# A hybrid decoder layer on one core: the last projections as channel pairs in seven products each

## The chip, the cores and the metric

The kernel runs on one NeuronCore of a Trainium2 chip (trn2). Its engines are TensorE (PE in the profile; its weight loads are PEld), VectorE (DVE), ScalarE (ACT), GpSimd (POOL) and SyncE (SP), which here issues all DMAs. The metric is the device time of one execution in microseconds, lower is better.

## What is computed

One layer on x, 1,024 positions by 1,024 channels, float32:

```
h = RMSNorm(x)
q,k,v,z_a | u,v_s,z_s | z_m,xBC,dt | gates = split(h @ W_in)
y_att = sliding_window_attention(q,k,v) * silu(z_a)      # 16 heads, window 128
y_sg  = u * (tril(W_s) LN(v_s) + b) * silu(z_s)          # chunks of 128, 8 channel groups
y_ssm = Mamba-2 scan of conv(xBC), dt; * silu(z_m); group RMSNorm   # 4 groups x 8 chunks
merged = sum_i sigmoid(gate_i) * (y_i @ W_br_i)
out = x + RMSNorm(merged @ W_out)
```

## The kernel before

Every float32 operand of a projection is split into a high and a low part in a rounded format (`hi` by a ScalarE cast, `lo` by a VectorE subtraction), and a product is three matmuls: hi x hi, hi x lo and lo x hi. `load_w` (line 76) loads and splits a tile of weights, `raw`, `whi`, `wlo`, with three buffers each. h lies transposed in `hT[0]` and `hT[1]` (high and low). A `ct_unit` (line 88) makes 128 output channels by 1,024 positions: two halves of 512 columns, each 8 k tiles x 3 matmuls into a buffer of `ps_mm`, of which there are three. A `tc_unit` (line 108) makes 128 positions by up to 416 channels, for eight row tiles.

`Stream` (line 133) queues such units and feeds them between other work: `fill(us)` issues steps for so many nominal us, `drain()` the rest; a half of a `ct_unit` counts as 5.2, a row tile of a `tc_unit` as 2.6. TensorE's order is the order in the program. The other engines' instructions and the DMAs are ordered by a planner when the program is built; each engine then runs its list in that order.

The stages are: (1) norm, transposes, and a first `tc_unit` with part of v_s, v and dt; (2) four groups of the scan, each six conv units drained and then a loop over eight chunks, where `decay`, `local`, `scan` and `sums` of the class `Mix` alternate with `st.fill`, and the fill is 5 gate units (6 in the last group) and the next group's four `z_unit`; z goes to two buffers `z2`, one for each half of the positions. (3) Attention in 32 steps with q, z_a and the last gates as fill. (4) A pool `gp`: v_s in three `tc_unit`, layernorm, then for each of eight channel groups `zs_unit`, `u_unit` and `sg_mix`. (5) Four branch passes of eight `ct_unit`, whose right side is y, read back from DRAM by `load_y`: DMA to `yraw` (four buffers), for the scan's y a scaling by `rsb` on POOL, then the cast and the subtraction (on POOL for tiles 4 and 5). The split tiles go to twelve slots; four of them lie in pool `py`, opened before stage 4, the others in `pz`, opened after h is freed. The first unit takes its k tiles as they come. (6) The output projection.

In `decay`, the wait that the change touches, VectorE makes the differences and ScalarE the exponential:

```
for j in range(8):
    V.tensor_scalar(seg[:, j, :], seg[:, j, :], acs[...], 0.0, op0=ALU.subtract, op1=ALU.min)
A.activation(seg, seg, AF.Exp)
```

## Time and profile before

| | |
|---|---|
| three runs, us | 1877.33, 1874.21, 1874.61; median 1874.61 |
| the profiled execution | 1877.33 us, of which the span from first to last instruction 1875.6 |
| mean granted TensorE clock | 0.997 |
| busy share PE / DVE / ACT / POOL | 98% / 55% / 32% / 20% |

Matmuls are pipelined: a busy time of 0.39 us for one of 512 columns is its latency, and its successor starts earlier. The idle time of an engine in a stretch is the stretch less its busy time. PE waits are those in which the engine stood still before an instruction; "<-" names what ended the wait.

### The profile page before, as it was taken

To read this page: it belongs to the slowest core of one execution; us is meant where nothing else is said; L and a number is where in the kernel's file an instruction comes from. 1 tells how busy PE (TensorE), PEld (TensorE's weight loads), DVE (VectorE), ACT (ScalarE), POOL (GpSimd) and SP (SyncE) were. 2 spreads that over 40 slices of the span, in tenths; PEclk is the share of its full clock that TensorE was granted. 3 is DMA by queue.
4 is the path that set the end of the run, shared out by engine and by line. 5 is a ranking of instruction groups with operands and counts; after the bars stand their busy time and mean duration, and the time that the engine had idled before them with its cause. 6 is when DMAs were issued, how large, how long until landed. Compare 5 with 4: busy or idle time off the path is not lost.

```text
span 1875.6 us, 24483 instructions
## 1 busy us (share of the span) xinstructions
PE 1837.7 (98%) x9649; PEld 1555.3 (83%) x9649; DVE 1025.5 (55%) x1653; ACT 599.2 (32%) x1181; POOL 379.0 (20%) x453
## 2 busy tenths in 40 slices
PE   7999999999999999999999999999999999999998
PEld 6888778887888788878888889988887888888898
DVE  6446764667366836685677664533336343534424
ACT  5233333423243324333555553211112021212121
POOL 1001320033003300242466654500003200000000
PEclk9999999999999999999999999999999999999999
DMA  6311441134113521243111114412224453534303
GB/s 207 104 46 56 141 146 45 57 128 154 62 46 102 166 76 46 90 141 114 34 58 46 57 51 157 142 45 68 68 68 152 151 180 94 198 92 135 100 24 135
DMA packets 86755, 186.55 MB, mean 99 GB/s; under 512 B 8528, under 2 KB 41584, under 8 KB 86384
## 3 DMA queue, kind: packets, MB, share of 16 engines
q1 hardware_dynamic: 86640, 184.98, 30.5%
q8 instruction: 76, 1.25, 0.3%
q14 instruction: 39, 0.32, 0.1%
HBM read 149.68 MB, written 35.27 MB: 99 GB/s over the span
## 4 chain that ended last, share of the span: by engine, by line
PE 80%; DVE 8%; issue 4%; ACT 3%; DMA 3%; POOL 2%; SPq 1%; DVEq 0%; POOLq 0%; ACTq 0%
PE ps_mm L100 22%; PE ps_mm L101 22%; PE ps_mm L102 22%; PE ps_mm L126 3%; PE ps_mm L127 3%; PE ps_mm L125 3%; DVE seg L413 1%; PE ps_ac L649 1%; POOL y L470 1%; ACT p L611 1%; DVE seg L438 1%; PE ps_ac L455 1%; DVE ssy L475 1%; ACT whi L82 1%; PE ps_ac L448 1%
## 5 line engine op out<-in xcount | busy, mean ns | idle before, releaser
L100 PE MATMUL ps_mm<-hT,whi 128*128 128x512 f32 x1552 | 612.4, 395 | 0.0
L102 PE MATMUL ps_mm<-hT,wlo 128*128 128x512 f32 x1552 | 604.7, 390 | 0.0
L101 PE MATMUL ps_mm<-hT,whi 128*128 128x512 f32 x1552 | 604.4, 389 | 0.0
L102 PEld LDWEIGHTS ps_mm<-hT,wlo 128*128 128x128 f32 x1552 | 291.3, 188 | 62.0
L100 PEld LDWEIGHTS ps_mm<-hT,whi 128*128 128x128 f32 x1552 | 291.5, 188 | 59.0 <-issue 1.4
L101 PEld LDWEIGHTS ps_mm<-hT,whi 128*128 128x128 f32 x1552 | 291.7, 188 | 57.8
L82 ACT CAST whi<-raw 128x1024 fp32r<-128x1024 f32 (+1 forms) x147 | 153.6, 1046 | 484.6 <-PE ps_mm L101 405.9
L83 DVE TENSOR_TENSOR wlo<-raw,whi 128x1024 fp32r<-128x1024 f32 (+1 forms) x145 | 193.5, 1335 | 200.9 <-ACT whi L82 200.9
L100 PE MATMUL ps_mm<-y,whi 128*128 128x512 f32 x512 | 200.0, 391 | 3.3 <-DVE mg L809 3.3
L101 PE MATMUL ps_mm<-y,whi 128*128 128x512 f32 x512 | 200.0, 391 | 0.6 <-DVE y L788 0.6
L102 PE MATMUL ps_mm<-y,wlo 128*128 128x512 f32 x512 | 199.8, 390 | 0.0
L379 DVE SCALAR_TENSOR_TENSOR acc<-xr,wcv,acc 128x512 f32<-128x512 f32 x144 | 111.3, 773 | 40.2 <-ACT acc L377 36.8
L437 POOL TENSOR_TENSOR y<-xg,dsk 128x512 f32<-128x512 f32 x32 | 38.1, 1202 | 463.0 <-issue 290.5
L100 PEld LDWEIGHTS ps_mm<-y,whi 128*128 128x128 f32 x512 | 96.5, 189 | 23.8 <-DVE mg L809 3.7
L101 PEld LDWEIGHTS ps_mm<-y,whi 128*128 128x128 f32 x512 | 96.4, 188 | 20.9 <-DVE y L788 1.0
L102 PEld LDWEIGHTS ps_mm<-y,wlo 128*128 128x128 f32 x512 | 96.5, 189 | 20.2
L812 DVE SCALAR_TENSOR_TENSOR tm<-gld,ps_mm 128x512 f32<-128x512 f32 x48 | 33.0, 687 | 134.4 <-PE ps_mm L102 134.3
L73 POOL TENSOR_TENSOR rso<-rso,mhalf_row 128x1 f32<-128x1 f32 x8 | 4.3, 542 | 402.5 <-DVE rso L72 402.5
L611 ACT ACTIVATE p<-s,mx 128x129 f32<-128x129 f32 x128 | 50.0, 392 | 101.4 <-DVE mx L607 101.4
L127 PE MATMUL ps_mm<-wlo,hT 128*128 128x256 f32 (+1 forms) x256 | 78.8, 308 | 3.4 <-DVE wlo L83 3.4
L125 PE MATMUL ps_mm<-whi,hT 128*128 128x256 f32 (+1 forms) x256 | 79.7, 311 | 1.5 <-ACT hT L260 1.5
L126 PE MATMUL ps_mm<-whi,hT 128*128 128x256 f32 (+1 forms) x256 | 79.0, 308 | 0.6 <-DVE hT L261 0.6
(184 smaller groups left out, 2583.8 us busy)
## 6 DMA issues: line engine op xcount, KB each, us to landing
seg<-acs_dr SPq DMA_DIRECT2D x32, 512.0 KB, 4.8
yraw<-y_dr SPq DMA_DIRECT2D x32, 512.0 KB, 5.2
raw<-in_w_br_dram SPq DMA_DIRECT2D x32, 512.0 KB, 4.3
gld<-gate_dr SPq DMA_DIRECT2D x32, 512.0 KB, 3.5
raw<-in_w_xbc_dram SPq DMA_DIRECT2D x24, 512.0 KB, 3.6
raw<-in_w_gate_dram SPq DMA_DIRECT2D x24, 512.0 KB, 3.6
gate_dr<-gt SPq DMA_DIRECT2D x48, 256.0 KB, 2.0
raw<-in_w_zm_dram SPq DMA_DIRECT2D x16, 512.0 KB, 5.0
```

The lines of the kernel that those rows point to most:

```text
L82: A.copy(hi, raw)
L83: eng.tensor_tensor(lo, raw, hi.bitcast(F32), op=ALU.subtract)
L100: T.matmul(ps, lhsT=whi[:, ks], rhs=rhs(0, kt, half), start=kt == 0, stop=False)
L101: T.matmul(ps, lhsT=whi[:, ks], rhs=rhs(1, kt, half), start=False, stop=False)
L102: T.matmul(ps, lhsT=wlo[:, ks], rhs=rhs(0, kt, half), start=False, stop=kt == KT - 1)
L125: T.matmul(o, lhsT=lhs(0, kt, tt), rhs=whi[:, ks], start=kt == 0, stop=False)
L126: T.matmul(o, lhsT=lhs(1, kt, tt), rhs=whi[:, ks], start=False, stop=False)
L127: T.matmul(o, lhsT=lhs(0, kt, tt), rhs=wlo[:, ks], start=False, stop=kt == KT - 1)
L379: V.scalar_tensor_tensor(acc, xr[:, k + f0:k + f0 + 512], wcv[:, ti, k:k + 1], acc, op0=ALU.mult, op1=ALU.add)
L437: G.tensor_tensor(d["y"], xg[g][:, :, cs], col(dsk, g), op=ALU.mult)
L611: A.activation(p[:, k, :], s4[:, k, :], AF.Exp, bias=mx[:, k:k + 1], accum_out=den[:, k:k + 1])
L812: V.scalar_tensor_tensor(tm, gt[0][:, fs], 1.0, ps, op0=ALU.add, op1=ALU.mult)
```

## The change

u and z_s, and the second twelve of the 24 gate tiles, are made after attention as 14 pairs of channel tiles. A pair is a product of 256 channels x 1,024 inputs with 1,024 x 1,024 positions, cut into 2 x 2 blocks, and the four output blocks come from seven block products in place of eight (Winograd's form of Strassen's method). The sums of weight blocks are made on POOL as weights come (T1 to T4), the sums of h once, on POOL, with their splits in new tiles S1, S2, S4 (the fourth overwrites a block of h), and the products are added up on VectorE, ScalarE and POOL. A new class `PairStream` issues one product of 12 matmuls at a time and prepares operands four products ahead.

The scan's loop gets 2 gate units and the four z units as fill (6 gates in the last group), in fills of 2.2 for 2.6. v_s moves into attention, where the last gates were, and goes through DRAM; its statistics are kept in `bst`, its norm is applied group by group when it is read back. The differences of `decay` move from VectorE to ScalarE, as a relu with a bias. `py` is opened after the last channel group, and the first three y are loaded while the gate pairs run; `yraw` has two buffers instead of four, and three y slots instead of four lie in `py`. `pz` lies where the S tiles, `ep` and h lay.

The diff, cut to its core:

```diff
+NGATE = 12
+NPY = 3
...
+    class PairStream:
+        AHEAD = 4
...
+        def _load(self, u):
+            raw = []
+            for k in range(2):
+                r = wp.tile([P, 1024], F32, name="raw", tag="raw", bufs=3)
+                nc.sync.dma_start(out=r, in_=self.units[u][0][k])
+                raw.append(r)
+            (r1, r2) = raw
+            self.raw[u] = {"B11": r1[:, 0:512], "B12": r1[:, 512:], "B21": r2[:, 0:512], "B22": r2[:, 512:]}
+        def _sum(self, b, out, x, y, op):
+            b[out] = self.pool.tile([P, 512], F32, name="ts", bufs=3)
+            G.tensor_tensor(b[out], b[x], b[y], op=op)
+        def _prepare(self, q):
+            u, i = divmod(q, 7)
+            while self.loaded <= u:
+                self._load(self.loaded)
+                self.loaded += 1
+            b = self.raw[u]
+            if i == 1:
+                self._sum(b, "T3", "B22", "B12", ALU.subtract)
+                self._sum(b, "T2", "T3", "B11", ALU.add)
+                self._sum(b, "T1", "B12", "B11", ALU.subtract)
+                self._sum(b, "T4", "T2", "B21", ALU.subtract)
+            src = b[("B11", "T2", "B21", "T3", "T1", "T4", "B22")[i]]
+            if q % 2 == 0:
+                self.slot = [wp.tile([P, 1024], F32R, name=n, tag=n, bufs=3) for n in ("whi", "wlo")]
+            hi, lo = (x[:, q % 2 * 512:q % 2 * 512 + 512] for x in self.slot)
+            A.copy(hi, src)
+            V.tensor_tensor(lo, src, hi.bitcast(F32), op=ALU.subtract)
+            self.ops[q] = hi, lo
+            if i == 6:
+                del self.raw[u]
+        def _step(self):
+            n = 7 * len(self.units)
+            if self.done >= n:
+                return None
+            while self.prepared < min(n, self.done + 1 + self.AHEAD):
+                self._prepare(self.prepared)
+                self.prepared += 1
+            u, i = divmod(self.done, 7)
+            hi, lo = self.ops.pop(self.done)
+            self.done += 1
+            if i == 0:
+                self.t = {}
+            t = self.t
+            o = psum(ps_mm, "mm")
+            for kt in range(4):
+                ks = slice(kt * P, (kt + 1) * P)
+                h0, h1 = (self.lhs(i, part, kt) for part in range(2))
+                T.matmul(o, lhsT=hi[:, ks], rhs=h0, start=kt == 0, stop=False)
+                T.matmul(o, lhsT=hi[:, ks], rhs=h1, start=False, stop=False)
+                T.matmul(o, lhsT=lo[:, ks], rhs=h0, start=False, stop=kt == 3)
+            def tmp(name):
+                t[name] = self.pool.tile([P, 512], F32, name="tp", bufs=6)
+                return t[name]
+            dst, evac = self.units[u][1]
+            def block(b, eng, x, y, op=ALU.add):
+                d = dst(b)
+                eng.tensor_tensor(d, x, y, op=op)
+                evac(b, d)
+            if i == 0:
+                A.copy(tmp("s1"), o)
+            elif i == 1:
+                V.tensor_tensor(tmp("u2"), t["s1"], o, op=ALU.add)
+            elif i == 2:
+                block(11, V, t["s1"], o)
+            elif i == 3:
+                V.tensor_tensor(tmp("u3"), t["u2"], o, op=ALU.add)
+            elif i == 4:
+                A.copy(tmp("s5"), o)
+                block(22, G, t["u3"], t["s5"])
+                G.tensor_tensor(t["u2"], t["u2"], t["s5"], op=ALU.add)
+            elif i == 5:
+                block(21, V, t["u3"], o, ALU.subtract)
+            else:
+                block(12, V, t["u2"], o)
+            return 2.8
...
             def first_evac(tt, o):
-                A.copy(vt[:, tt, :], o[:, 0:384])
+                vt = xp.tile([P, 384], F32, name="vt", bufs=3)
+                A.copy(vt, o[:, 0:384])
                 V.tensor_tensor(dtr[:, tt, :], o[:, 384:416], dtb, op=ALU.add)
+                V.bn_stats(bst[:, tt, 0, 0:6], vt[:, 0:256])
+                nc.sync.dma_start(out=vs_dr[:, tt, 0:256], in_=vt[:, 0:256])
+                nc.sync.dma_start(out=v_dr[:, tt, :], in_=vt[:, 256:384])
...
-            nc.sync.dma_start(out=v_dr, in_=vt)
...
                     A.activation(ea, ea, AF.Exp)
                     self.d[c]["ea"] = ea
                 for j in range(8):
-                    V.tensor_scalar(seg[:, j, :], seg[:, j, :], acs[:, c, g * 8 + j:g * 8 + j + 1], 0.0,
-                                    op0=ALU.subtract, op1=ALU.min)
-                A.activation(seg, seg, AF.Exp)
+                    A.activation(seg[:, j, :], seg[:, j, :], AF.Relu, scale=-1.0,
+                                 bias=acs[:, c, g * 8 + j:g * 8 + j + 1])
+                A.activation(seg, seg, AF.Exp, scale=-1.0)
...
-            st.add(*[gate_unit(next(gates), mp) for _ in range(5)])
-            if g == 3:
-                st.add(*[gate_unit(next(gates), mp) for _ in range(1)])
-            else:
+            st.add(*[gate_unit(next(gates), mp) for _ in range(6 if g == 3 else 2)])
+            if g < 3:
                 st.add(*[z_unit(g + 1, j) for j in range(4)])
             mix.decay(0)
             st.fill(10.4)
@@ -498,16 +617,27 @@
                     mix.local(i)
                     if i + 1 < NB:
                         mix.decay(i + 1)
-                st.fill(2.6)
+                st.fill(2.2)
                 if 3 <= i:
                     mix.sums(i - 3)
                 if 1 <= i <= NB:
                     mix.scan(i - 1)
-                st.fill(2.6)
...
+    def vs_unit(qd):
+        def evac(tt, o):
+            vt = vsp.tile([P, 256], F32, name="vst", bufs=3)
+            A.copy(vt, o)
+            V.bn_stats(bst[:, tt, qd, 0:6], o)
+            nc.sync.dma_start(out=vs_dr[:, tt, qd * 256:(qd + 1) * 256], in_=vt)
+        return tc_unit([t["w_vs"][qd - 1][i] for i in range(2)], h_tc, evac, 256)
...
-                        st.add(*[gate_unit(i, ac) for i in gates])
+                        st.add(*[vs_unit(qd) for qd in range(1, 4)])
...
+    es7 = ExitStack()
+    sop = es7.enter_context(tc.tile_pool(name="sop", bufs=1, side="right", reuse_waits="tile"))
+    ep = es7.enter_context(tc.tile_pool(name="ep", bufs=1, side="right", reuse_waits="tile"))
+    sums = {i: [sop.tile([P, 4, 512], F32R, name=f"S{i}{part}") for part in range(2)] for i in (1, 2, 4)}
+    def blk(part, i, j):
+        return hT[part][:, j * 4:(j + 1) * 4, i * 512:(i + 1) * 512]
+    def h_pair(i, part, kt):
+        if i in (1, 4, 6):
+            return sums[{1: 2, 4: 1, 6: 4}[i]][part][:, kt, :]
+        return blk(part, *{0: (0, 0), 2: (0, 1), 3: (1, 0), 5: (1, 1)}[i])[:, kt, :]
+    def split(hi, lo, src):
+        A.copy(hi, src)
+        V.tensor_tensor(lo, src, hi.bitcast(F32), op=ALU.subtract)
+    pst = PairStream(ep, h_pair)
+    with tc.tile_pool(name="bp", bufs=1, reuse_waits="tile") as bp:
+        s3 = [bp.tile([P, 512], F32, name=f"s3{kt}") for kt in range(4)]
+        for kt in range(4):
+            r = {}
+            for i in range(2):
+                for j in range(2):
+                    r[i, j] = bp.tile([P, 512], F32, name=f"r{i}{j}", bufs=2)
+                    G.tensor_tensor(r[i, j], blk(0, i, j)[:, kt, :].bitcast(F32),
+                                    blk(1, i, j)[:, kt, :].bitcast(F32), op=ALU.add)
+            s1, s2, s4 = (bp.tile([P, 512], F32, name=f"s{i}") for i in (1, 2, 4))
+            G.tensor_tensor(s1, r[1, 0], r[1, 1], op=ALU.add)
+            G.tensor_tensor(s2, s1, r[0, 0], op=ALU.subtract)
+            G.tensor_tensor(s3[kt], r[0, 0], r[1, 0], op=ALU.subtract)
+            G.tensor_tensor(s4, r[0, 1], s2, op=ALU.subtract)
+            for i, x in ((1, s1), (2, s2), (4, s4)):
+                split(sums[i][0][:, kt, :], sums[i][1][:, kt, :], x)
+            st.fill(10.4)
         st.drain()
-
-
-    py = ctx.enter_context(tc.tile_pool(name="py", bufs=1, reuse_waits="tile"))
+        for kt in range(4):
+            split(blk(0, 1, 0)[:, kt, :], blk(1, 1, 0)[:, kt, :], s3[kt])
...
+        for c in range(NB):
+            V.bn_aggr(mv[:, c, :], bst[:, c, :, 0:6])
+        V.tensor_scalar(rsv, mv[:, :, 1], EPS, None, op0=ALU.add)
+        G.tensor_tensor(rsv, rsv, mhalf.broadcast_to([P, NB]), op=ALU.pow)
...
+        def zu_unit(g):
+            def dst(b):
+                half, which = b // 10 - 1, zs if b % 10 == 1 else us
+                if which is zs:
+                    zs[g, half] = gp.tile([P, 512], F32, name="zs", bufs=4)
+                else:
+                    us[g, half] = gp.tile([P, 512], F32, name="us", bufs=2)
+                return which[g, half]
+            def evac(b, src):
+                if b in (11, 21):
+                    th = gp.tile([P, 512], F32, name="th", bufs=2)
+                    A.activation(th, src, AF.Tanh, scale=0.5)
+                    V.scalar_tensor_tensor(src, th, 1.0, src, op0=ALU.add, op1=ALU.mult)
+                if b in (12, 21):
+                    half = 0 if b == 12 else 1
+                    V.scalar_tensor_tensor(zs[g, half], us.pop((g, half)), 0.5, zs[g, half],
+                                           op0=ALU.mult, op1=ALU.mult)
+            return [t["w_zu"][g][k] for k in range(2)], (dst, evac)
+        def sg_load(g):
+            gs = slice(g * P, (g + 1) * P)
+            vg = gp.tile([P, NB, P], F32, name="vg", bufs=2)
+            nc.sync.dma_start(out=vg, in_=vs_dr[:, :, gs])
+            w = gp.tile([P, P], F32, name="sgw", bufs=2)
+            nc.sync.dma_start(out=w, in_=t["sg_wT"][:, g, :])
+            bb = gp.tile([P, P], F32, name="sgb", bufs=2)
+            bcast_load(bb, t["sg_b"][gs])
+            G.affine_select(w, w, pattern=[[1, P]], compare_op=ALU.is_ge, fill=0.0, base=0, channel_multiplier=-1)
+            G.tensor_tensor(vg, vg, mv[:, :, 0:1].broadcast_to([P, NB, P]), op=ALU.subtract)
+            V.tensor_tensor(vg, vg, rsv.unsqueeze(2).broadcast_to([P, NB, P]), op=ALU.mult)
+            sg[g] = vg, w, bb
...
+        def gate_pair(n):
+            def tile_(b):
+                return ep.tile([P, 512], F32, name="tp", bufs=6)
+            def evac(b, gt):
+                A.activation(gt, gt, AF.Tanh, scale=0.5)
+                i, half = NGATE + 2 * n + b % 10 - 1, b // 10 - 1
+                nc.sync.dma_start(out=gate_dr[i, :, half * 512:(half + 1) * 512], in_=gt)
+            return [t["w_gp"][n][k] for k in range(2)], (tile_, evac)
+        pst.add(*[zu_unit(g) for g in range(8)])
+        ngp = (24 - NGATE) // 2
+        pst.add(*[gate_pair(n) for n in range(ngp)])
         for g in range(9):
             if g < 8:
-                st.add(zs_unit(g), u_unit(g))
-                st.drain()
+                sg_load(g)
+                pst.fill(2.8 * 3)
             if g > 0:
                 sg_mix(g - 1)
-    ph1.close()
-
-
-    pz = ctx.enter_context(tc.tile_pool(name="pz", bufs=1, reuse_waits="tile"))
-    merged = [pz.tile([P, S], F32, name=f"mg{i}") for i in range(8)]
+            if g < 8:
+                pst.fill(2.8 * 4)
...
-        return [(py if k < 4 else pz).tile([P, S], F32R, name=f"y{i}", tag=f"y{i}_{k}") for i in range(2)]
+        return [(py if k < NPY else pz).tile([P, S], F32R, name=f"y{i}", tag=f"y{i}_{k}") for i in range(2)]
...
-        raw = py.tile([P, S], F32, name="yraw", bufs=4)
+        raw = py.tile([P, S], F32, name="yraw", bufs=2)
...
+    for n in range(NPY):
+        ys[n] = load_y(n)
+    pst.drain()
+    es7.close()
+    ph1.close()
+    pz = ctx.enter_context(tc.tile_pool(name="pz", bufs=1, reuse_waits="tile"))
+    merged = [pz.tile([P, S], F32, name=f"mg{i}") for i in range(8)]
...
-        return ct_unit(t["w_br"][un * 8 + dd], rhs, evac, (4, 5, 6, 7, KT) if un == dd == 0 else (KT,))
-
-    for n in range(8):
+        return ct_unit(t["w_br"][un * 8 + dd], rhs, evac, (3, 4, 5, 6, 7, KT) if un == dd == 0 else (KT,))
+    for n in range(NPY, 8):
```

## Rows read from the trace of the kernel before

**Rows 1.** The page's first part: busy time, share and instructions of each engine.

```profile
PE 1837.7 (98%) x9649; PEld 1555.3 (83%) x9649; DVE 1025.5 (55%) x1653; ACT 599.2 (32%) x1181; POOL 379.0 (20%) x453
```

**Rows 2.** The page's chain that ended last, shares of the span by engine.

```profile
PE 80%; DVE 8%; issue 4%; ACT 3%; DMA 3%; POOL 2%; SPq 1%; DVEq 0%; POOLq 0%; ACTq 0%
```

**Rows 3.** Timeline of TensorE (start, us, instruction): two plain stretches, first and last.

```profile
699.72 0.39 PE L101 MATMUL ps_mm<-hT,whi 128*128 128x512 f32 x1
...
705.84 0.39 PE L101 MATMUL ps_mm<-hT,whi 128*128 128x512 f32 x1
...
1194.82 0.28 PE L125 MATMUL ps_mm<-whi,hT 128*128 128x256 f32 x1
...
1197.94 0.28 PE L127 MATMUL ps_mm<-wlo,hT 128*128 128x256 f32 x1
```

**Rows 4.** Busy us by stage: stretch, length, PE, PEld, DVE, ACT, POOL, clock.

```profile
184.00:264.00 80.00, 78.12 (x469) 62.06 (x469) 62.45 (x116) 26.75 (x49) 30.31 (x25) 1.00 0.48 147
...
1140.00:1157.50 17.50, 17.50 (x101) 15.39 (x100) 5.97 (x10) 6.13 (x9) 8.48 (x13) 1.00 0.23 77
...
1233.00:1418.00 185.00, 185.00 (x866) 154.85 (x866) 56.83 (x75) 24.51 (x32) 0.00 (x0) 1.00 0.20 64
1431.00:1460.00 29.00, 25.55 (x104) 20.65 (x105) 18.77 (x13) 6.09 (x6) 17.61 (x7) 0.94 0.75 266
```

**Rows 5.** TensorE's waits: waiting line, releaser, us in total, times, longest.

```profile
PE ps_tr L426 <- ACT ssum L482: 8.8, 12, 1.0
PE ps_mm L127 <- DVE wlo L83: 3.4, 1, 3.4
PE ps_mm L100 <- DVE mg L809: 3.3, 1, 3.3
```

**Rows 6.** VectorE timeline, one chunk; groups of ScalarE (busy, mean ns, idle).

```profile
802.65 1.65 DVE L413 TENSOR_SCALAR seg<-seg,acs 128x128 f32<-128x128 f32 x8
...
L611 ACT ACTIVATE p<-s,mx 128x129 f32<-128x129 f32 x128 | 50.0, 392 | 101.4 <-DVE mx L607 101.4
...
L415 ACT ACTIVATE seg<-seg 128x1024 f32<-128x1024 f32 x32 | 33.9, 1058 | 77.9 <-DVE seg L413 77.9
...
L430 ACT COPY btok<-ps_tr 128x128 f32<-128x128 f32 x32 | 8.5, 266 | 48.5 <-DVE gtm L428 48.5
```

**Rows 7.** Single lines (ns least, median, most); a group of the page (busy, mean).

```profile
L471 DVE TENSOR_TENSOR y<-y,z x32: 680/1104/1521, 198.9 to 856.8; 128x512 f32<-128x512 f32 x32
...
L463 DVE TENSOR_TENSOR st<-st,ps_ac x24: 666/678/689, 206.2 to 845.8; 128x512 f32<-128x512 f32 x24
...
L83 DVE TENSOR_TENSOR wlo<-raw,whi 128x1024 fp32r<-128x1024 f32 (+1 forms) x145 | 193.5, 1335 | 200.9 <-ACT whi L82 200.9
```

**Rows 8.** The chain that ended last, in the pass of the channel groups.

```profile
1394.54 1.78 PE ps_ac L726 x16
```

**Rows 9.** Timeline of TensorE at the entry to the branches.

```profile
1431.16 0.50 PE L101 MATMUL ps_mm<-y,whi 128*128 128x512 f32 x1 [0.59 <-DVE y L788]
...
1453.56 0.59 PE L100 MATMUL ps_mm<-y,whi 128*128 128x512 f32 x1 [3.29 <-DVE mg L809]
...
1456.93 0.54 PE L102 MATMUL ps_mm<-y,wlo 128*128 128x512 f32 x1
```

**Rows 10.** Instructions on tile yraw: count, ns least/median/most, first, last start.

```profile
L787 ACT CAST y<-yraw x32: 1038/1048/1059, 1176.6 to 1687.5; 128x1024 fp32r<-128x1024 f32 x32
L788 DVE TENSOR_TENSOR y<-yraw,y x30: 1200/1219/3418, 1177.7 to 1689.2; 128x1024 fp32r<-128x1024 f32 x30
L785 POOL TENSOR_TENSOR yraw<-yraw,rsb x16: 2376/2408/3384, 1174.2 to 1461.9; 128x1024 f32<-128x1024 f32 x16
L788 POOL TENSOR_TENSOR y<-yraw,y x2: 2475/2660/2845, 1420.0 to 1422.5; 128x1024 fp32r<-128x1024 f32 x2
...
DMA to landing us min/median/max: 3.4/5.2/10.0
```

**Rows 11.** The chain that ended last, in the first stage.

```profile
33.09 3.47 DMA xt<-in_x_dram
```

More of the change, by code (lines that the diff above doesn't have):

```diff
@@ L731, in sg_mix @@
                 ytf = yt.rearrange("p j s -> p (j s)")
-                V.tensor_tensor(ytf, ytf, zs[g][:, half * 512:(half + 1) * 512], op=ALU.mult)
+                V.tensor_tensor(ytf, ytf, zs.pop((g, half)), op=ALU.mult)
                 nc.sync.dma_start(out=y_dr[24 + g, :, half * 512:(half + 1) * 512], in_=ytf)
-        st.add(*[vs_unit(qd) for qd in range(1, 4)])
-        st.fill(5.2)
-        for c in range(NB):
-            nc.sync.dma_start(out=vs[c][:, 0:256], in_=v_dr[:, c, 0:256])
-            V.bn_stats(bst[:, c, 0, :], vs[c][:, 0:256])
@@ L768, in hybrid_kernel @@
+    py = ctx.enter_context(tc.tile_pool(name="py", bufs=1, reuse_waits="tile"))
     spare = {}
```

101 lines of the change are left out of this document (47 added, 54 removed).

## The prediction, made before the change was run

> **What bounds the kernel now.** I read the page first. TensorE is busy 98% of the span and the next engine 55% [rows 1], and the chain that ended last lies 80% on TensorE [rows 2]. A matmul's busy time is a latency that overlaps its neighbour's, so a full TensorE row alone says little; the next view was therefore the start times in a plain stretch of projections. 27 matmuls of 512 columns start in 705.84 - 699.72 = 6.12 us, 0.227 us each [rows 3], and each matmul of that size in the projections and branches costs this much of the path as long as TensorE waits for nobody. The windows by stage show where it does wait [rows 4]: nowhere in the pass that makes u and z_s (185.00 of 185.00), 1.9 us in a scan (one of four is shown), 3.4 us around 1445. TensorE's own list of waits names them [rows 5]: 8.8 us in the four scans for ScalarE's copy of a sum, 3.4 us at the v_s units, 3.3 us in the first branch. So what counts is (a) matmuls taken away, at 0.227 us, (b) waits of TensorE taken away, (c) waits put in. Other engines' work is free until it makes a wait.
>
> **Products: -38.1 us.** u, z_s and twelve gates are 28 tiles, each 2 halves of 24 matmuls. As 14 pairs in seven products of 12 they take 14 x 84 = 1,176 matmuls instead of 14 x 96 = 1,344: 168 x 0.227 = 38.1 us less. Operands keep their size (128x128 against 128x512), so I keep the pace.
>
> **Scan: -5 us (bounds -8.8 to +3).** Per chunk VectorE loses eight subtractions, 1.65 us for the eight as they run back to back [rows 6]. Now ScalarE's exponential waits for them, 77.9 us in total [rows 6], and the small copy that TensorE waits for [rows 5] is on the same engine. Afterwards ScalarE does both steps itself. Its price is not in the trace: from below a 128x128 copy is 0.27 us, from above an activation with a bias column and a sum is 0.39 us on 129 columns [rows 6], which gives 2.1 to 3.1 us a chunk; I take 0.30 each, since the upper row also accumulates. VectorE is busy 62 of 80 us in a scan and ScalarE 27 [rows 4]; 64 x 0.3 = 19 us bring ScalarE to 46, so there is room. Filler moves out of the scan (12 half units in place of 13); that is done elsewhere and costs nothing in itself. One wait is put in on paper: the z units of the next group now start in chunk 3 instead of 8, and their second halves cannot be evacuated until chunk 7 has read the old second half. Counting the fills at 2.2, two such results hold two of the three ps_mm buffers from chunk 4 to 8, the third serves the rest, and the next buffer is asked for after chunk 7's scan. I price it at nothing; with the scan a chunk late it is one evacuation a group, under 2 us. Of the 8.8 us I take 5.
>
> The Trainium skill speaks against this move (ScalarE: Activation LUTs, section "Rules for kernel authors"): relu belongs on VectorE, which is faster per element. By that the step would be 2.4 us against 1.65 a chunk; no run here yet shows the operation on ScalarE.
>
> **Entry to the pairs: -3.4 and +3 us (0 to 10).** The wait at the v_s units goes, since they now fill attention. In its place come the sums of h: POOL makes 32 of 128x512, each half of the 2.41 us of its 1,024-wide product [rows 10], 38.5 us. TensorE's cover is the rest of v_s. At step 28 of attention the queue holds 7.8 + 62.4 nominal us and seven steps take 36.4, so 33.8, or 13 row tiles, are left, each 24 matmuls at 0.12 us (1197.94 - 1194.82 for 26 [rows 3]): 37.4 us, plus the first product, which needs no sum, 2.7 us. POOL is half busy at attention's end (8.48 of 17.50 [rows 4]), so some sums can start early, if the planner places them so; the splits into the S tiles must wait for attention's memory. With 10 us done early there is no wait; with none, T3 and T2 (2.4 us), a cast and a split behind them and VectorE's splits in between, 5 to 10 us. SyncE's load of v_s for group 0 waits for the last v_s write, and the pairs' weights may stand behind it.
>
> **Inside a u/z_s pair: +2 us over all eight (0 to 55).** TensorE: 84 x 0.227 + 18/16 x 1.78 for mixing and bias [rows 8] = 21.0 us. VectorE: 20 steps of 512 at 0.68 (seven splits, five sums with a PSUM input, four of gating, four of mixing) and one 1,024-wide scaling at 1.22: 14.8 us [rows 7, 10]. ScalarE: 11 steps at about half of 1.05 [rows 10]. POOL: 6 x 1.2 + 2.4 = 9.6. TensorE is still the longest, if VectorE's times hold. They need not: with two SBUF inputs y<-y,z takes 0.68 to 1.52 us, median 1.10, and the wide split of y 1.20 to 3.42, while sums with a PSUM input stay within 0.67 and 0.69 [rows 7, 10]. What differs is whether POOL runs beside them. 13 of the 20 steps and the wide one have two SBUF inputs. If half of their delay strikes, as the median of y<-y,z has it, VectorE needs 14.8 + 6.5 = 21.3, 0.3 over TensorE. If they are hit only in proportion, as the weight splits are (1.335 on average against 1.22, 9%, with POOL busy a fifth of the span [rows 1, 7, 10], so some 23% with POOL busy half), 17.1. I take the second, being the larger count, and 2 us for single late operands; they are prepared four products, 10.9 us, ahead.
>
> The Trainium skill calls this a lock (SBUF — State Buffer, section "Who interferes with whom"): a VectorE instruction with two SBUF inputs and a GpSimd one that reads SBUF exclude each other for a whole instruction. The rows agree in kind: 0.84 us more is most of a 1.2 us POOL operation.
>
> In the six gate pairs VectorE has 12 of those steps, 8.2 us, against 19.0 of TensorE: nothing.
>
> **Entry to the branches: +15 us (0 to +20).** Now four of the first eight y are split long before, and the other four lie in four yraw buffers, already scaled; only casts and splits remain, and TensorE waits 0.59 us [rows 9]. After the change three are ready, two lie in the only two yraw buffers, and their targets in pz overlie h and the S tiles, which TensorE reads until the last products. So y5 can be loaded only when y3 or y4 is split. From the end of the pairs (0): y3 is split at 0 to 2.5; then load 5.2 (least 3.4), scaling on POOL 2.41, cast 1.05, split on POOL 2.66 [rows 10]: y5 at 1.2 + 11.3 = 12.5. y7, in y5's or y6's buffer: load, scaling, cast and a split of 1.22 on VectorE, 9.9: 22.4 (17.6 to 25.9). TensorE then does the last 6 matmuls, 1.4 us, and ends the first unit at 23.8 instead of 48 x 0.227 = 10.9: 12.9 us of waiting (8.1 to 16.4), in two gaps of several us. The present 3.29 us gap shows what a gap adds: the eight starts after it lie 0.42 us apart, the lower level of 1.2 GHz, before the pace is 0.227 again [rows 9]; 1.6 us a gap. 12.9 + 3.2 - 0.6 is 15.5; I take 15. The 3.3 us block of VectorE at y8 stays. Nothing is added only if y5 to y7 find buffers earlier than I see.
>
> **First stage: +1.5 us (0 to 4).** One write of v becomes 16, on the queue that feeds x, whose load is on the chain there with 3.5 us [rows 11]; eight statistics join VectorE.
>
> **Sum.** -38.1 - 5 - 3.4 + 3 + 2 + 15 + 1.5 = -25.0. The profiled execution took 1877.33 (span 1875.6 and 1.7 around it) and is the slowest of the three runs: 1852.3. From their median, 1874.61, it is 1849.6. I say 1850.
>
> **Rivals.** (A) As above, 0.56. (B) The branch entry is hidden and the scans lose all waits: 1850 - 15 - 3.8 = 1831. For it: scaling of y began at 1174 before, some 240 us ahead [rows 10]. Against it: two buffers. 0.14. (C) VectorE becomes the pairs' bound: with all 13 steps at 1.52 and the wide one at 3.42 a pair takes 27.9 us against 21.0, 8 x 6.9 - 2 = +53: 1903. It ends slower than before once a pair takes over 21.0 + 26.6/8 = 24.3 us, three quarters of those delays. For it y<-y,z; against it the weight splits, and that nothing but chance puts POOL's work beside VectorE's. 0.10. The Trainium skill's lock (SBUF — State Buffer, same section) is this case when every such pair of instructions meets. (D) ScalarE becomes the scan's pace: 8 x 0.39 + 1.06 in one queue with steps that wait for others, 1 us a chunk over today: 32 us more and the 5 not won, 1887 at full, 1871 at half. For it the 77.9 us that ScalarE already waits in; against it 46 of 80 us. 0.12, mostly at half or less. The Trainium skill's rule on relu (ScalarE: Activation LUTs) would come out here. (E) Nothing is won: sums late by 10, branch entry 20, pairs 10 and scans as now: 1875. 0.08.
>
> **Chances and range.** A measurement of this kernel tells about 0.2% (3.7 us) from no change. Faster: A, B, most of D, half of E, 0.84; same: the rest of E, 0.05; slower: C and the end of D, 0.11. The range leaves out C, D's end and the low end of B: 1830 to 1874. A alone is 1839 to 1861.
>
> **What would show it.** 1,176 pair matmuls 0.227 us apart and 21 us from one mixing to the next; 24.3 or more is C. No wait for ssum's copy: the scan step is right; scans longer than now with less filler: D. No gap before the first product that reads an S tile: the sums were in time. Two gaps of 3 to 8 us in the first branch unit, before y5 and y7: the branch step is right; none: B. The prediction is wrong if TensorE waits elsewhere, above all inside the pairs.

## The result, and the profile after

The changed kernel takes 1918.69 us (median of 4 runs, 1915.50 to 1924.31) where the kernel before takes 1875.97 (4 runs beside it): a ratio of 1.0231, 95% interval 1.0200 to 1.0261. It is slower, against a forecast of 1850 us with a range of 1830 to 1874. The profiled execution took 1924.31 us with a span of 1922.6, 47.0 us longer than the span before.

The first part of its page, and its row of TensorE's granted clock in 40 slices:

```profile
PE 1827.9 (95%) x9481; PEld 1540.4 (80%) x9481; DVE 1101.1 (57%) x1546; ACT 724.5 (38%) x1551; POOL 570.9 (30%) x570
...
PEclk9999999999999999999999989999997999999999
```

TensorE has 9649 - 9481 = 168 instructions less than in [rows 1], just those of the products, but its share fell from 98% to 95%, and two slices show a lower clock where none did. The products' pace, from TensorE's timeline inside a pair:

```profile
1200.99 0.39 PE L247 MATMUL ps_mm<-hT,whi 128*128 128x512 f32 x1
...
1211.89 0.39 PE L247 MATMUL ps_mm<-hT,whi 128*128 128x512 f32 x1
```

48 matmuls in 10.90 us are 0.227 us each, as in [rows 3]. So the saving is there, and more than twice as much is lost to something else. TensorE's waits after (waiting line, releaser, us in total, times, longest), against [rows 5]:

```profile
PE ps_tr L602 <- ACT btok L551: 13.9, 8, 3.4
PE ps_mm L105 <- ACT y L964: 12.3, 3, 7.2
PE ps_mm L130 <- DVE bst L637: 11.8, 2, 7.4
PE ps_tr L375 <- DVE hh L367: 10.4, 3, 7.4
PE ps_mm L130 <- ACT whi L87: 9.8, 1, 9.8
PE ps_mm L247 <- DVE us L259: 6.0, 4, 2.1
```

Only the fourth row (the first norm) was there before at about this size. The others name four places: the scan (btok), the entry to the pairs (the v_s units' L130, for evacuations and for a weight), the pairs (L247), and the branches (L105). The windows by stage of the changed kernel (columns as in [rows 4]), one scan, the entry to the pairs, the pairs, the entry to the branches:

```profile
184.00:264.00 80.00, 75.68 (x455) 59.99 (x453) 51.07 (x70) 37.77 (x92) 29.93 (x24) 0.96 0.38 119
1095.00:1165.00 70.00, 44.27 (x249) 40.55 (x250) 35.10 (x49) 18.76 (x37) 49.06 (x34) 0.80 0.23 67
1165.00:1350.00 185.00, 179.00 (x841) 148.43 (x840) 150.88 (x179) 52.26 (x92) 100.93 (x64) 0.98 0.32 103
1444.00:1480.00 36.00, 21.33 (x66) 15.24 (x65) 11.32 (x9) 8.89 (x10) 16.48 (x8) 0.72 0.62 221
```

A stage loses by its waits and by the lower clock level after them, so I put both in one number. For every two neighbouring TensorE instructions of a trace I take the time between their starts, less the median of that time for the same line and shape; the sum over a stage is its excess. The medians add up to 1811.7 us before and 1776.0 after, 35.7 less: the products. The excess, in us, worked out so for every profiled execution below (in the kernel before, "to pairs" is its v_s units and "pairs" its u and z_s tiles; "to branches" are the first 41 us behind the pairs):

```
                      first  scans  attn  to pairs  pairs  to branches  later
before                 11.4   21.0   4.5     6.4    -0.1      6.5       -0.4
after                  16.2   32.9   6.8    30.2    16.1     21.4        8.4
e1_scan_decay          14.8   43.1   8.3    29.3    19.4     18.5        8.1
e2_entry_sums          15.2   27.6   6.6     0.1    20.2     18.2        7.7
e3_pair_vg_early       11.6   28.1   6.7    30.4    16.9     20.9        8.8
e4_branch_order         9.8   28.8   8.2    29.4    17.7     13.2       12.6
e5_scan_fills          13.9   14.9   6.9    30.4    18.0     17.6        8.4
e6_pair_vg_pool        11.1   28.2   8.2    29.4    11.6     19.0        8.1
e7_pair_no_sums        14.9   29.0   6.8    25.2     6.9     19.3        7.8
e8_yraw_four           12.0   28.4   8.0    30.3    17.5      9.0       -0.5
e9_pair_sums_vec       13.3   28.3   8.2    26.6    15.6     20.2        7.0
e10_all                10.7   13.6   8.3     0.1     5.9      9.9       -0.5
e11_all_sums_vec       11.1   14.7   8.4     0.0    10.1     10.3       -0.5
e12_all_order          11.9   15.6   8.4     0.1     4.1      4.2       -0.5
e13_scan_gates_only    15.7   34.2   8.3    29.0    17.9     18.2        7.3
e14_all_decay          16.0   24.0   8.3     0.1     5.2      4.3       -0.5
```

After less before: +4.8, +11.9, +2.3, +23.8, +16.2, +14.9, +8.8, together 82.7; less 35.7 that is the 47.0 us. Where an experiment left a stage as it is in the changed kernel, attention, the way to the pairs and the later passes repeat within 2 us. The first stage lies between 9.8 and 16.2, the scans between 27.6 and 32.9, the pairs between 16.1 and 20.2, and the way to the branches between 17.6 and 21.4, so smaller differences there say nothing. The trace of the changed kernel has the least of these values for the pairs and the greatest for the branches.

### The profile page after: what moved, and what is told of

Same layout as the page of the kernel before. It is cut to its first block, busy times and chain, and to the rows that moved or that the text cites. A ratio compares the mean times of both kernels' runs of the same rounds, so it can differ in the third digit from the quotient of the medians.

```text
span 1922.6 us, 24786 instructions
## 1 busy us (share of the span) xinstructions
PE 1827.9 (95%) x9481; PEld 1540.4 (80%) x9481; DVE 1101.1 (57%) x1546; ACT 724.5 (38%) x1551; POOL 570.9 (30%) x570
## 5 line engine op out<-in xcount | busy, mean ns | idle before, releaser
L105 PE MATMUL ps_mm<-hT,whi 128*128 128x512 f32 x1104 | 436.6, 395 | 0.8 <-DVE z L317 0.8
L107 PE MATMUL ps_mm<-hT,wlo 128*128 128x512 f32 x1104 | 430.2, 390 | 0.0
L106 PE MATMUL ps_mm<-hT,whi 128*128 128x512 f32 x1104 | 430.1, 390 | 0.0
L87 ACT CAST whi<-raw 128x1024 fp32r<-128x1024 f32 (+1 forms) x119 | 124.1, 1043 | 338.1 <-PE ps_mm L106 317.0
L105 PEld LDWEIGHTS ps_mm<-hT,whi 128*128 128x128 f32 x1104 | 207.4, 188 | 44.3 <-issue 2.5
L107 PEld LDWEIGHTS ps_mm<-hT,wlo 128*128 128x128 f32 x1104 | 207.3, 188 | 44.0
L106 PEld LDWEIGHTS ps_mm<-hT,whi 128*128 128x128 f32 x1104 | 207.7, 188 | 40.9
L88 DVE TENSOR_TENSOR wlo<-raw,whi 128x1024 fp32r<-128x1024 f32 (+1 forms) x117 | 152.2, 1302 | 117.7 <-ACT whi L87 117.6
L105 PE MATMUL ps_mm<-y,whi 128*128 128x512 f32 x512 | 202.8, 396 | 12.3 <-ACT y L964 12.3
L106 PE MATMUL ps_mm<-y,whi 128*128 128x512 f32 x512 | 203.2, 397 | 7.1 <-DVE y L965 3.8
L105 PEld LDWEIGHTS ps_mm<-y,whi 128*128 128x128 f32 x512 | 98.0, 191 | 34.5 <-ACT y L964 14.1
L130 PE MATMUL ps_mm<-whi,hT 128*128 128x256 f32 (+1 forms) x256 | 83.0, 324 | 25.7 <-DVE bst L637 11.8
L247 PE MATMUL ps_mm<-hT,whi 128*128 128x512 f32 x224 | 89.8, 401 | 10.3 <-DVE us L259 6.0
L534 ACT ACTIVATE seg<-seg,acs 128x128 f32<-128x128 f32 x256 | 80.9, 392 | 28.2 <-DMA seg<-acs_dr 28.1
L249 PE MATMUL ps_mm<-hT,wlo 128*128 128x512 f32 x224 | 88.6, 396 | 0.0
```

What stands on the lines that cost most here:

```text
L87: A.copy(hi, raw)
L88: eng.tensor_tensor(lo, raw, hi.bitcast(F32), op=ALU.subtract)
L105: T.matmul(ps, lhsT=whi[:, ks], rhs=rhs(0, kt, half), start=kt == 0, stop=False)
L106: T.matmul(ps, lhsT=whi[:, ks], rhs=rhs(1, kt, half), start=False, stop=False)
L107: T.matmul(ps, lhsT=wlo[:, ks], rhs=rhs(0, kt, half), start=False, stop=kt == KT - 1)
L130: T.matmul(o, lhsT=lhs(0, kt, tt), rhs=whi[:, ks], start=kt == 0, stop=False)
```

## The experiments

Each kernel differs from the changed one as its diff shows. Times stand against 1918.7 us; those of the kernel before, run beside them, were 1875.6 to 1875.9.

**The scan.** First the relus were put back as subtractions (e1_scan_decay).

```
-   A.activation(seg[:, j, :], seg[:, j, :], AF.Relu, scale=-1.0, bias=acs[...])
-   A.activation(seg, seg, AF.Exp, scale=-1.0)
+   V.tensor_scalar(seg[:, j, :], seg[:, j, :], acs[...], 0.0, op0=ALU.subtract, op1=ALU.min)
+   A.activation(seg, seg, AF.Exp)
```

> The scan's segment subtraction is back on VectorE (tensor_scalar, then Exp without the sign), the fills stay at 2.2; all else as in the changed kernel (1918.7 us). Theory: the eight relus of a chunk stand at the head of ScalarE's in-order queue, wait there for the segment's transfer (28.1 us over 19 waits), and btok and the ssum copy wait behind them, which is the 2.4 to 3.4 us wait of TensorE in each group (13.9 us over 8). Then the excess of the four scans falls from 33 us to 21 to 24 us, the waits for btok go, and the time is 1907 to 1911 us. Rival: the smaller fills (2.2 for 2.6) leave chunks with too little work between them, whichever engine subtracts. Then the waits move to a releaser on VectorE and the time stays at 1915 to 1922 us.

1929.7 us (ratio 1.0293, 1.0275 to 1.0310), 11 us slower still; the waits for btok came to 17.0 us where they had been 13.9. My theory fell: the relus help. A wait in the changed kernel, from the timelines of TensorE, ScalarE and VectorE:

```profile
212.67 0.60 PE L547 MATMUL ps_tr<-ident,xg 128*128 128x128 f32 x4
216.46 0.58 PE L602 MATMUL ps_tr<-ones,ssy 128*128 128x1 f32 x2 [3.18 <-ACT btok L551]
```

```profile
207.80 2.45 ACT L534 ACTIVATE seg<-seg,acs 128x128 f32<-128x128 f32 x8 [2.42 <-DMA seg<-acs_dr]
...
213.61 0.69 ACT L534 ACTIVATE seg<-seg,acs 128x128 f32<-128x128 f32 x2 [2.27 <-DMA seg<-acs_dr]
214.21 0.61 ACT L594 ACTIVATE sqj<-y 128x512 f32<-128x512 f32 x1
...
216.14 0.27 ACT L551 COPY btok<-ps_tr 128x128 f32<-128x128 f32 x1 [0.21 <-DVE gtm L549]
```

```profile
214.86 1.05 DVE L596 TENSOR_REDUCE ssy<-sqj 128x128 f32<-128x512 f32 x1 [1.56 <-ACT sqj L594]
215.83 0.28 DVE L549 TENSOR_TENSOR gtm<-ps_tr,gmask 128x128 f32<-128x128 f32 x1
```

Between the transposes (L547) and the sum (L602) of this chunk there is no projection at all, where the kernel before has a half unit in every chunk. ScalarE waits for a transfer, VectorE for ScalarE, and nothing covers it. A chunk's two fills of 2.2 give 4.4 nominal us and a half unit costs 5.2, so in some chunks the first fill issues nothing. In TensorE's trace those with a sum behind their transposes are the fourth and the fifth chunk of each group: eight places in the four groups, and the eight waits for btok lie two in each group. Two runs tested that; the first changes the fills and, so that the work lasts, the gate tiles, the second the gate tiles alone.

```
-   st.add(*[gate_unit(next(gates), mp) for _ in range(6 if g == 3 else 2)])
+   st.add(*[gate_unit(next(gates), mp) for _ in range((3, 3, 4, 6)[g])])    # NGATE = 16
-   st.fill(2.2)      # twice in each chunk; e5_scan_fills only
+   st.fill(2.6)
```

> The scan's fills are 2.6 again (one half unit in each chunk), and the groups have 3, 3, 4 and 6 gate tiles for 2, 2, 2 and 6, so that the work lasts; the relus stay on ScalarE. Four gate tiles thereby go back from two pairs (2 x 19.1 us) to plain tiles (4 x 10.9 us), which costs 5.4 us. All else as in the changed kernel (1918.7 us). Theory: with fills of 2.2 one chunk in six has no half unit between its steps, the segment's buffer and TensorE's transposes then come a half unit too early, and all of the scans' extra 11.6 us comes from there. Then the waits for btok go, the excess of the scans falls from 33 to some 20 us, and the time is 1908 to 1913 us. Rival: ScalarE's eight relus in a row delay btok at any pace of the chunks. Then the waits stay, and the time is 1921 to 1926 us.

> The changed kernel with 3, 3, 4 and 6 gate tiles in the scans, and the fills left at 2.2; so the z units start later, as in the run with fills of 2.6, and the pace is that of the changed kernel. Theory of the pace: the two chunks a group without a half unit stay, the excess of the scans stays at 27 to 32 us, and the time is 1917 to 1923 us. Rival: the z units' second halves, which cannot be evacuated before chunk 7, made the waits. Then the excess falls to some 15 us, and the time is 1904 to 1910 us.

With both: 1906.3 us (1.0166, 1.0150 to 1.0182), 12.4 less, although the four gate tiles that go back to plain form cost 24 matmuls, 5.4 us; the excess of the scans is 14.9, and of TensorE's waits in the scans these are left, none for btok:

```profile
PE ps_tr L547 <- ACT ssum L603: 2.5, 5, 1.1
PE ps_mm L105 <- DVE z L317: 1.1, 2, 0.6
```

With the gates alone: 1925.3 us (1.0262, 1.0238 to 1.0286), excess 34.2, btok 15.7 us in 8 waits. So it is the pace of the fills, not the chunk in which the z units start.

**The entry to the pairs.** POOL's timeline there, the first and the last sums, and what ScalarE waits for from 1075 to 1135:

```profile
1080.51 5.03 POOL L839 TENSOR_TENSOR r<-hT,hT 128x512 f32<-128x512 f32 x4
...
1127.22 1.70 POOL L845 TENSOR_TENSOR s<-r,s 128x512 f32<-128x512 f32 x1
```

```profile
ACT S L828 <- POOL s L842: 18.3, 4, 5.0
ACT S L828 <- POOL s L843: 8.7, 4, 2.3
...
ACT S L828 <- POOL s L845: 7.0, 4, 2.3
```

POOL begins after attention's last step and needs 48 us. ScalarE's queue:

```profile
1088.07 0.62 ACT L828 CAST S<-s 128x512 fp32r<-128x512 f32 x1 [3.67 <-POOL s L842]
1088.60 0.37 ACT L636 COPY vst<-ps_mm 128x256 f32<-128x256 f32 x1
1091.03 0.63 ACT L828 CAST S<-s 128x512 fp32r<-128x512 f32 x1 [2.06 <-POOL s L843]
...
1099.30 0.62 ACT L828 CAST S<-s 128x512 fp32r<-128x512 f32 x1 [4.71 <-POOL s L842]
1099.83 0.36 ACT L636 COPY vst<-ps_mm 128x256 f32<-128x256 f32 x1
1102.19 0.62 ACT L828 CAST S<-s 128x512 fp32r<-128x512 f32 x1 [2.00 <-POOL s L843]
1102.71 1.04 ACT L87 CAST whi<-raw 128x1024 fp32r<-128x1024 f32 x1
```

TensorE's longest wait in this stage:

```profile
1103.81 0.58 PE L130 MATMUL ps_mm<-whi,hT 128*128 128x256 f32 x1 [9.79 <-ACT whi L87]
```

The evacuations (L636) of v_s tiles run only when the cast ahead of them has its sum from POOL; at 1099.83 TensorE had stood still for some 6 us. The cast of the last v_s weights (L87) stands behind two such casts, and it is what TensorE's longest wait is for. So the v_s units, meant as the cover of the sums, are held up by them.

```
-   G.tensor_tensor(r[i, j], ...)      # and s1, s2, s3, s4: 32 in all
+   V.tensor_tensor(r[i, j], ...)
```

> The 32 sums of h blocks at the entry to the pairs run on VectorE instead of POOL; all else as in the changed kernel (1918.7 us). Theory: POOL needs 49 us for its sums (1.29 to 1.7 us each), and the casts and splits that wait for it stand in ScalarE's and VectorE's in-order queues ahead of the evacuations of the v_s projections, so TensorE starves at POOL's pace. With 32 sums at some 0.7 us on VectorE (22 us of its idle time) the excess of 1040 to 1165 us falls from 30 us to 8 to 14 us, and the time is 1897 to 1904 us. Rival: it is the amount of work in front of the evacuations, or the transfers of the weights, and not POOL's pace. Then 22 us more on VectorE leave the waits in place and the time is 1912 us or more.

1888.8 us (1.0077, 1.0051 to 1.0104): 29.9 less, more than the theory said, and the excess at this place is 0.1. The rival fell: VectorE makes the sums besides its own work and TensorE does not wait. The run doesn't tell apart POOL's 1.29 us a sum and the 0.4 us that a split beside it takes longer (1.1 us for 0.69).

**The pairs.** VectorE's groups from 1165 to 1350 (busy, mean ns, idle before and its releaser), changed kernel:

```profile
L225 DVE TENSOR_TENSOR wlo<-ts,whi 128x512 fp32r<-128x512 f32 x33 | 33.1, 1014 | 0.3 <-ACT whi L224 0.3
...
L887 DVE SCALAR_TENSOR_TENSOR zs<-us,zs 128x512 f32<-128x512 f32 x16 | 19.6, 1224 | 1.0
...
L901 DVE TENSOR_TENSOR vg<-vg,rsv 128x1024 f32<-128x1024 f32 x6 | 10.7, 1791 | 19.2 <-POOL vg L900 19.2
...
L259 DVE TENSOR_TENSOR zs<-tp,ps_mm 128x512 f32<-128x512 f32 x15 | 10.2, 678 | 3.7 <-PE ps_mm L249 3.7
```

Two suspects: steps with two SBUF inputs take 1.0 to 1.2 us, while the sum with a PSUM input takes 0.678; and VectorE stands for POOL's vg. Four runs:

```
e3   the DMAs of sg_load(g + 1) issued right after sg_mix(g - 1), the arithmetic left where it was
e6   -  V.tensor_tensor(vg, vg, rsv...)        +  G.tensor_tensor(vg, vg, rsv...)
e7   the four _sum calls left out; T1 to T4 replaced by B11, B12, B22, B12 (other numbers come out)
e9   -  G.tensor_tensor(b[out], b[x], b[y])    +  V.tensor_tensor(b[out], b[x], b[y])
```

> In the pairs, the three transfers of each spatial gate (vg, its matrix, its bias) are issued four products before their arithmetic and not directly ahead of it; all else as in the changed kernel (1918.7 us). Theory: VectorE stands at vg's normalisation (22.3 us over 7 waits) for POOL, which stands for vg's transfer (25.5 us over 3), and with it the evacuations that release TensorE. Then both waits go, the period of a pair falls from 22.9 us to 21.2 to 21.8, and the time is 1907 to 1912 us. Rival: VectorE and POOL slow each other (VectorE's subtraction at 1.0 us for 0.68, POOL's sum at 1.6 for 1.3), so that VectorE is full either way. Then the period stays at 22.4 us or more, and the time at 1914 to 1920 us.

1919.2 us (1.0233, 1.0215 to 1.0252), excess 16.9. This tested nothing: the order in which the program writes the transfers is not the order in SyncE's queue. In e3 vg still stood behind the weights there, and POOL's waits for it are those of the changed kernel (25.7 us for 25.5).

> In the pairs, the second step of vg's normalisation runs on POOL like the first, so that VectorE no longer waits there; all else as in the changed kernel (1918.7 us). (The earlier emission of vg's transfers left their place in SP's queue as it was, behind the weights, and so tested nothing of this.) Theory: VectorE's 22 us at vg are what makes every second pair's evacuation late. Then the period of a pair falls from 22.9 to 21.3 to 21.8 us, and the time is 1908 to 1913 us. Rival: the exclusion of VectorE and POOL makes VectorE full, and POOL has 1.9 us more in each pair. Then the period stays at 22.4 us or more, and the time at 1915 to 1925 us.

1909.3 us (1.0187, 1.0163 to 1.0212), excess 11.6 for 16.1, and 22.0 us from one mixing (the matmuls with sgw) to the next where the changed kernel takes 22.9 (the mean of six, from the starts of L908): the wait at vg is a part, not the whole. VectorE's splits of T sums rose to 1.37 us here, and it waits 12.2 us for a tile (`us`) from POOL instead.

> POOL's four sums of weight blocks in each pair are left out, and the products take plain weight blocks in their place (the products of the pairs are other numbers, as many and as long); all else as in the changed kernel (1918.7 us). Theory of the exclusion: of POOL's 101 us of 185 the sums are 50 us; without them VectorE's splits fall from 1.0 us towards 0.75, the period of a pair falls from 22.9 to 21.1 to 21.6 us, and the time is 1904 to 1910 us. Rival (VectorE's wait at vg alone): POOL reaches vg no earlier, since it waits there for the transfer. Then the period stays at 22.4 us or more, and the time at 1914 to 1920 us.

1902.7 us (1.0144, 1.0129 to 1.0159), 21.1 us from mixing to mixing for 22.9, excess 6.9, of which 5.0 is one late evacuation among the gate pairs. Two groups in the same window:

```profile
L225 DVE TENSOR_TENSOR wlo<-raw,whi 128x512 fp32r<-128x512 f32 x60 | 56.2, 958 | 9.6 <-ACT whi L224 9.6
...
L887 DVE SCALAR_TENSOR_TENSOR zs<-us,zs 128x512 f32<-128x512 f32 x14 | 9.7, 690 | 1.2 <-DVE zs L884 0.5
```

Without the sums L887 takes 0.69 us in place of 1.22, but the splits (L225), which I expected near 0.75, still 0.96: POOL is busy 58.5 us of the window with its other steps. VectorE's busy time in the window fell from 150.9 to 134.3 us, though its own work was the same; its wait at vg from 19.2 to 12.3.

> In the pairs, the four sums of weight blocks run on VectorE and not on POOL; all else as in the changed kernel (1918.7 us). Leaving them out gave a pair of 21.1 us for 22.3 and 1902.7 us. Theory: the pairs lose by the exclusion (VectorE's steps take 1.0 us for 0.68 while POOL adds) and by POOL's pace, not by the amount of work. VectorE then has 2.7 us more work in a pair and gets some 3 to 4 us back on its other steps, the period is 21.1 to 21.6 us, and the time 1903 to 1911 us. Rival: VectorE is nearly full by its own work (18 of 22.3 us a pair), and 2.7 us more make it the bound. Then the period is 22.3 us or more, and the time 1917 to 1930 us.

1911.6 us (1.0192, 1.0176 to 1.0209), excess 15.6, 22.25 us from mixing to mixing: neither theory quite. VectorE's other steps sped up (L887 0.68), but its busy time stayed at 151.9, since the sums took what the exclusion gave back, and it still waited 21.5 us for POOL's vg. So neither the wait at vg (e6) nor POOL's sums on VectorE (e9) mends the pairs alone; without the sums (e7) the pace is TensorE's own, though a wait at vg is left. How the loss divides between the wait and the slower steps, these runs do not show.

**The branches.** Timelines of SyncE, TensorE (its longest wait) and POOL at the entry (the bracket says how long the engine stood still and what ended it):

```profile
1449.03 2.55 SPq L957 DMA_DIRECT2D yraw<-y_dr  x2
...
1463.42 1.41 SPq L957 DMA_DIRECT2D yraw<-y_dr  x2
```

```profile
1459.91 0.79 PE L105 MATMUL ps_mm<-y,whi 128*128 128x512 f32 x1 [7.21 <-ACT y L964]
```

```profile
1456.44 4.65 POOL L962 TENSOR_TENSOR yraw<-yraw,rsb 128x1024 f32<-128x1024 f32 x2 [5.21 <-DMA yraw<-y_dr]
...
1468.70 2.34 POOL L962 TENSOR_TENSOR yraw<-yraw,rsb 128x1024 f32<-128x1024 f32 x1 [5.31 <-DMA yraw<-y_dr]
```

The transfers go two at a time, and the next two 14 us later. Two mends:

```
e4   order = (2, 0, 1, 3): attention's tiles, which L962 doesn't scale, in the first pass
e8   -  NPY = 3, yraw bufs=2, xt2 in a buffer of its own
     +  NPY = 2, yraw bufs=4, xt2 in yraw's buffers
```

> The first pass of the branch projection takes attention's eight tiles, which need no scaling by the row norms on POOL, and the two scaled passes come second and third; all else as in the changed kernel (1918.7 us). Theory: at the entry each tile goes in a row through a transfer (5 us), POOL's scaling (2.4 to 2.7 us), ScalarE's cast and the split, with two buffers for the raw tile; without POOL's step the excess of 1452 to 1480 us falls from 21 us to 10 to 14 us, and the time is 1906 to 1913 us. Rival: the two raw buffers alone set the pace (a transfer is issued only when the split of the tile two before it is done). Then a tile still takes as long as transfer, cast and split, 5 to 6 us for two tiles, the excess stays at 18 us or more, and the time at 1914 to 1922 us.

> Four buffers for the raw branch tiles in place of two, with two tiles (not three) kept ready before the branches for the room; all else as in the changed kernel (1918.7 us). Theory: a tile's transfer is issued only when the split of the tile two before it is done, so transfer (5 us), scaling (2.5 us), cast and split follow each other; with four buffers the transfers run ahead, the waits of the later passes (8.7 us) go, and the excess at the entry falls from 21 to 13 to 18 us: 1902 to 1908 us. Rival: POOL's scaling (2.4 to 2.7 us a tile, after its last work for the pairs) and the casts set the pace. Then the entry stays at 20 us or more, only the later passes gain something, and the time is 1911 to 1918 us.

The order alone: 1912.2 us (1.0199, 1.0182 to 1.0216); the entry went from 21.4 to 13.2, as forecast, but the scaled tiles now come in later passes and lose 12.6 there for 8.4. Four buffers: 1898.6 us (1.0122, 1.0100 to 1.0144), 20.1 less, more than expected; the entry 9.0, the later passes nothing, though one tile less was ready. TensorE's waits from 1425 to 1700 with four:

```profile
PE ps_mm L105 <- ACT y L964: 2.6, 1, 2.6
PE ps_mm L106 <- DVE y L965: 2.6, 2, 1.8
PE ps_mm L106 <- POOL y L965: 1.1, 2, 0.7
```

**Together.** e10_all has the entry's sums on VectorE, the fills of 2.6 with the gate tiles of e5, four raw buffers, and vg's normalisation on ScalarE:

```
-   G.tensor_tensor(vg, vg, mv[:, :, 0:1]..., op=ALU.subtract)
-   V.tensor_tensor(vg, vg, rsv..., op=ALU.mult)
+   for c in range(NB):     # nmr = -mean * rsv, once
+       A.activation(vg[:, c, :], vg[:, c, :], AF.Identity, scale=rsv[:, c:c + 1], bias=nmr[:, c:c + 1])
```

e11_all_sums_vec adds the pair sums on VectorE, e12_all_order the order of e4, and e14_all_decay is e12 with the diff of e1.

> Four mends together on the changed kernel (1918.7 us): the entry's sums on VectorE (measured alone 1888.8 us), the fills of 2.6 with 16 plain gate tiles (1906.3), four raw branch buffers (1898.6), and vg's normalisation on ScalarE in eight activations, which takes 1.9 us a pair from POOL and 1.8 from VectorE. Theory: the four places are apart in time and each wait is local, so the gains add: 1918.7 - 29.9 - 12.4 - 20.1 = 1856, less 3 to 9 us for vg, 1847 to 1853 us; by TensorE's paces (1778 us and an excess of some 12 + 15 + 7 + 2 + 11 + 9) it is 1836 us. So 1836 to 1853 us, below the kernel before. Rival: the waits hide behind one another, or the mends collide at the entry to the pairs and the branches. Then 1862 us or more.

> The four mends together and, besides, the four sums of each pair on VectorE. Theory of the exclusion: 5 to 9 us below the four mends alone, since POOL is left with two steps a pair. Rival: VectorE's own work decides: the same or slower than the four mends alone.

> The four mends together and, besides, attention's tiles in the first pass of the branches. Theory: of the 9 us that are left at the branches' entry with four buffers, POOL's scaling is part, and 3 to 6 us go. Rival: with four buffers the transfers and the casts set the entry, and the time is that of the four mends within 2 us.

> The best version (the four mends and attention's tiles first, 1839.1 us) with the scan's subtraction back on VectorE. The prediction's step: the relus on ScalarE are worth 5 us (0 to 9) at an even pace: 1840 to 1848 us. By what they gave at the uneven pace: 11 us, 1850 us. Rival: at an even pace ScalarE's eight relus cost TensorE as much as VectorE's subtractions: within 2 us of 1839.

e10: 1846.2 us (0.9845, 0.9829 to 0.9861). The gains add; the pairs lose 5.9. e11: 1849.2 us (0.9858, 0.9844 to 0.9871): the rival held; from mixing to mixing it is 21.1 us for 21.5, but the first S products wait for their operands (2.8 and 1.7 us), so nothing is won. e12: 1839.1 us (0.9810, 0.9791 to 0.9828), the best, 36.7 us under the kernel before; with four buffers the order no longer costs later passes anything. The page of e12:

```profile
PE 1804.0 (98%) x9505; PEld 1526.3 (83%) x9505; DVE 1104.2 (60%) x1551; ACT 742.3 (40%) x1601; POOL 485.7 (26%) x518
...
PEclk9999999999999999999999999999999999999999
```

e14: 1852.7 us (0.9869, 0.9849 to 0.9889), one run of four 1844.9. The scans' excess is 24.0 for 15.6, and TensorE's wait there for ssum's copy 7.8 us in 8 waits; 4.1 us of the rest lie in the first stage, which this edit doesn't touch. At an even pace the relus are worth some 8 us.

## Why the prediction was wrong

By the excess of the profiled execution four terms of the sum failed: the scan (16.9 us off), the entry to the pairs (24.2), the pairs (14.2) and the later passes, which are not in the sum (8.8). The rest is 8 us.

- **Products, -38.1.** Right: 168 matmuls less at 0.227 us; by the medians -35.7; the 2.4 us between are not traced.
- **Scan, -5.** The result was +11.9. The step that failed is the sentence "Filler moves out of the scan (12 half units in place of 13); that is done elsewhere and costs nothing in itself". It counted half units and not how they fall on chunks. The relus themselves were rightly judged: eight take 2.45 us back to back, 0.31 each, and at the even pace (e5) the wait for ssum's copy is 2.5 us for 8.8 [rows 5] and the scans' excess 14.9, 6.1 under the kernel before. At the even pace the z units, which I did examine, cost a wait of 1.1 us. The Trainium skill's rule that relu belongs on VectorE (ScalarE: Activation LUTs, "Rules for kernel authors") holds for the single step here, 2.45 us against 1.65 [rows 6]. Followed in e14 it costs the scans 8.4 us.
- **Attention, nothing.** +2.3, and 6.6 to 8.4 in every changed kernel for 4.5 before. v_s as its fill was not priced; 2.3 us of TensorE's waits there are one for VectorE's yst (L788).
- **Entry to the pairs, -3.4 and +3.** The wait at the v_s units did not go (-3.4); the sums made it larger: +23.8. The failed step is the sentence that TensorE's cover is the rest of v_s. I set 38.5 us of POOL beside 37.4 us of TensorE and took them as independent, naming one cast and one split behind T3 and T2. But 12 casts and 12 splits that wait for POOL share ScalarE's and VectorE's queues with v_s's evacuations and the casts of its weights. The bound of 10 us let TensorE lose only what comes behind the cover. Smaller: a sum took 1.26 us and more, not 1.2, and none started early.
- **Pairs, +2.** +16.2. From one mixing to the next it took 22.9 us against 21.0, in turns 21.4 to 21.6 and 23.0 to 25.0. The mechanism of rival C was at work, but C as stated did not come: VectorE is 82% busy (150.88 of 185.00) and not the bound. The failed step is to take VectorE's mean work, 17.1 of 21 us, for the test: at 82%, with steps that double in a row and a wait of some 3 us at vg in the same queue, its evacuations come late (L247 <- us, zs). That these two together make every second one late is argued; e7 and e10 show only that with less of them it goes, or nearly. I had left POOL's wait for vg's transfer out, and put the exclusion too low: 23% by my count, 45 to 80% by L225 and L887.
- **Entry to the branches, +15.** +14.9 (11 to 15, as this stage repeats), and by the cause named: two raw buffers; with four the excess falls to 9.0. There were two large gaps, 7.2 and 3.7 us, before y5 and y7 as forecast, and one of 2.7 between.
- **Later passes, nothing.** +8.8. Left out altogether: the second pass too reads tiles through the two buffers, which e8 shows by its -0.5.
- **First stage, +1.5.** +4.8, inside what this stage varies by.

Of 1850, then, the term that came from counting instructions held, and so did the one worked out tile by tile through its buffers. The three where I compared totals, half units or busy times of engines, did not. With those places mended the kernel takes 1846.2 us. That this is near 1850 is in part chance: that kernel has four raw buffers in place of the forecast wait at the branches, and two pairs fewer.

## What to carry to other kernels

Work given to an idle engine, to be hidden behind other work (its cover), is only hidden if no in-order queue that the cover itself needs holds a step waiting for it: list, per queue, what stands behind each step that waits. When filler is cut, look at which step then has none, not at the total. Before two buffers replace four, follow one tile through transfer, arithmetic and release, in every later pass as well.
